# More projection steps between transposes and values in two groups of attention, and the first input tiles loaded among the first weights

## The chip, the cores and the metric

The kernel runs on one core of a Trainium2 chip. The metric is device microseconds of one execution, as the median of several. A profiled execution of the same program gives a trace, with the time and the length of every instruction on each engine. TensorE is written PE (its weight loads PEld), VectorE DVE, ScalarE ACT, GpSimd POOL, and SyncE, which issues most of the transfers here, SP.

## The reference

One layer of a streaming encoder is applied to a prompt of 2048 rows and to a sample of 32 rows that has a cache of 2048 past rows; the model width is 1024. What matters here is its first half:

```
proj = x @ w_in                     # q | k | v | forget logits | B | C | h
logf = log_sigmoid(f_logit + b_f);  c = cumsum(logf)
s = q k^T / 8 + c_q - c_k           # 8 heads of 64, causal
attn = softmax(s) @ v
conv_out = B * dwconv3_causal(C * h)
x = LayerNorm(alpha * x + concat(attn, conv_out) @ w_out)
```

Then follow a gated ConvFFN and a second LayerNorm. Keys, values, log forget values and the states of the convolutions are outputs too. All is fp32.

## The kernel before, in words

**Precision.** A product of fp32 matrices is made of three matmuls: each operand is split into a rounded high half (`hi`, L75 to L82, on ACT, DVE or POOL) and the rest (`lo`, L85, always DVE), and `three` (L87) issues high x high (L89), high x low (L90) and low x high (L91). Tiles are named in pairs: xh and xl (input), wh and wl (weights), ph and pl (probabilities).

**Stages.** The prompt is cut into 4 groups of 512 rows. For each group j, `qkv(j)` (L242) makes keys, queries and values, and `conv(j, half)` (L377) the gated short convolution; `attend(j)` (L528) is the attention of group j's queries over groups 0 to j. `attend_sample`, `cache_gates` and `cache_keys` serve the sample. Then come the output projection with the first norm (`mix`), and the feed-forward. The change touches only the first part, about 0 to 500 us.

**The order by hand.** These functions are Python generators. Each `yield` gives the cost of the stretch just issued, roughly in microseconds of TensorE. `merge` (L1526) drives `together` (L1508): it is given streams with a total each, always resumes the stream with the smallest (cost so far / total), and drops a stream that has ended. So the totals set how fast the streams go against each other: attention in group 0 has the total 24 beside 97 for the projection of group 1, and a yield of 1 in attention lets 97/24 = 4.04 of projection through. What a generator issues between two yields stays together in the program's order; the tile framework may still move an instruction past others where it expects them to wait. Four merges follow each other (L1462 to L1466): group 0's projection alone; attention 0 beside projection 1 and the first cache steps; attention 1 beside projection 2 and the rest of the cache steps; then attentions 2 and 3 with further work.

**A projection step.** `product` (L217) accumulates one 128-column half of a weight piece over the 8 input tiles, and yields 1.3 after every second tile: 6 matmuls of 512 columns. `values` inside `qkv` (L291) yields 1.3 for 12 matmuls of 256 columns. Projection plus `conv(j, 0)` costs 97.1 in all.

**Attention.** For head h and pair 0 or 1 (two blocks of 128 queries each), `scores` (L556) makes score tiles in PSUM, which DVE moves out with the row maximum (L506, L510); `softmax` (L518) takes exp on ACT (L523) and scales on POOL (L525). `values` (L571) then transposes the probabilities on TensorE (`transposed`, L581), splits them (ACT, DVE), and multiplies them by v (L605). The values of a pair come after the scores of the next pair. `nk` is the number of key blocks, 4 j + 2 pair + 2: 2 and 4 in group 0, 6 and 8 in group 1. Up to three sets are transposed ahead (a set is at most four transposes into one PSUM tile), then comes the yield on L593, which the change alters: the merge puts projection there while ACT and DVE make ph and pl. Then each step of values has its own yield (L607).

**The start.** `fetch` (L178) loads, casts and splits the weights in halves of four k tiles. The first half is cut into three transfers (k tile 0, k tile 1, k tiles 2 and 3), in the buffer `wr`. `load_x` (L147) loads the 8 input tiles: for group 0 the first two go into `xr` (2 buffers), the others into the score buffers, which nobody uses yet. All these transfers are issued from SP, one after the other: first the three weight cuts, then the eight tiles, three small constants, then the second half of the weights. TensorE starts with k tile 0.

Of the kernel before, what the change touches and what calls it, by code (L numbers as in the profile page):

```python
# [7 lines left out]
F32 = mybir.dt.float32  # L8
# [9 lines left out]
TS = 32  # L18
# [4 lines left out]
GT = 512  # L23
# [9 lines left out]
def width(j):  # L33
    return GT + TS if j == 0 else GT
# [27 lines left out]
class Kernel:  # L62
# [84 lines left out]
    def load_x(self, j, xp, wide=None):  # L147

        n = width(j)
        self.x = []  # L150
        for k in range(KD):
            if wide and k >= 2:
                if k % 3 == 2:
                    big = wide.tile([128, 2176], F32, tag="p", bufs=5, name="xw")
                r = big[:, n * ((k + 1) % 3):n * ((k + 1) % 3) + n]
            else:
                r = xp.tile([128, GT + TS], F32, tag="xr", bufs=2, name="xr")[:, :n]
            self.dma(r, self.i["xt0"][k] if j == 0 else self.i["xt"][j - 1, k])
            a = xp.tile([128, 640], F32R, tag="xh", bufs=8, name="xh")[:, :n]
            b = xp.tile([128, 640], F32R, tag="xl", bufs=8, name="xl")[:, :n]  # L160
            self.hi(a, r, "act")
            self.lo(b, r, a)
            self.x.append((a, b))
# [14 lines left out]
    def fetch(self, upto):  # L178

        wp = self.wp  # L180
        for s in range(len(self.halves), min(upto, 2 * len(self.order))):
            src, w = self.order[s // 2]
            cuts = [slice(0, 4)] if s else [slice(0, 1), slice(1, 2), slice(2, 4)]
            r = wp.tile([128, 4, 264], F32, tag="wr", bufs=2, name="wr")[:, :, :w]
            a, b = (wp.tile([128, 1152], F32R, tag=t, bufs=3, name=t)[:, :4 * w].rearrange("p (k c) -> p k c", k=4)
                    for t in ("wh", "wl"))
            for c in cuts:
                self.dma(r[:, c], src[:, 4 * (s % 2) + c.start:4 * (s % 2) + c.stop])
                self.hi(a[:, c], r[:, c], "pool" if s else "dve")
                self.lo(b[:, c], r[:, c], a[:, c])  # L190
            self.halves.append([(a[:, k], b[:, k]) for k in range(4)])
# [50 lines left out]
    def qkv(self, j, pools, acc):  # L242
        nc = self.nc
        xp, wp, ev = pools
        n = width(j)
        st = self.stores
        if j == 0:
            self.fetch(1)
        self.load_x(j, xp, None if j else self.at)

# [277 lines left out]
    def attend(self, j, at, mmp, ptp, op):  # L528
# [42 lines left out]
        def values(h, pair, ps, vv):  # L571
            st.flush()
            o = op.tile([128, 256], F32, tag="o", name=f"o{j}o")
            nk = 4 * j + 2 * pair + 2
            def transposed(m):
                last = m == nk // 2 - 1
                pt = ptp.tile([128, GT], F32, tag="pt", name=f"pt{j}t")
                blocks = [(0, 2 * m, 0), (1, 2 * m, 128)]
                blocks += [(1, 2 * m + 1, 256)] if last else [(0, 2 * m + 1, 256), (1, 2 * m + 1, 384)]
                for e, kt, col in blocks:  # L580
                    nc.tensor.transpose(pt[:, col:col + 128], ps[e][:, 128 * kt:128 * kt + 128], self.ident)  # L581
                w = 384 if last else GT
                ph = at.tile([128, GT], F32R, tag="ph", bufs=4, name="ph")
                pl = at.tile([128, GT], F32R, tag="pl", bufs=4, name="pl")
                with self.tc.high_priority(self.HP):
                    self.hi(ph[:, :w], pt[:, :w], "act")
                    self.lo(pl[:, :w], pt[:, :w], ph[:, :w])
                return ph, pl

            nxt = [transposed(0)]  # L590
            for m in range(1, min(3, nk // 2)):
                nxt.append(transposed(m))
            yield 0.43 * len(nxt)  # L593
            for m in range(nk // 2):
                last = m == nk // 2 - 1
                if m + 3 < nk // 2:
                    nxt.append(transposed(m + 3))
                ph, pl = nxt.pop(0)
                order = [(0, ph), (1, ph), (1, pl), (0, pl)]
                for s, (x, pp) in enumerate(order):  # L600
                    kt = 2 * m + x
                    part = last and x == 1
                    oo = o[:, 128:256] if part else o
                    cs = slice(256, 384) if part else slice(256 * x, 256 * x + 256)
                    nc.tensor.matmul(oo, vv[kt // 4][:, kt % 4, :], pp[:, cs],  # L605
                                     start=(m == 0 and s == 0), stop=(last and s == 3))
                yield 0.87 if m + 3 < nk // 2 else 0.43  # L607
            t0 = at.tile([128, 256], F32, tag="ot", bufs=2, name="ot")[:64]
            nc.scalar.copy(t0, o[64:128])
            t1 = at.tile([128, 256], F32, tag="os", bufs=2, name="os")[:64]  # L610
            nc.vector.tensor_tensor(out=t1, in0=o[0:64], in1=t0, op=ALU.add)
            r = slice(64 * (h % 2), 64 * (h % 2) + 64)
            st(self.MX[j][2 * pair:2 * pair + 2, r, h // 2, :].rearrange("t p c -> p t c"),
                     t1.rearrange("p (t c) -> p t c", t=2))
# [813 lines left out]
    def run(self):  # L1428
        tc, nc = self.tc, self.nc
        with ExitStack() as top:  # L1430
# [5 lines left out]
            with ExitStack() as st:  # L1436
                pool = lambda nm, bufs=1, **kw: st.enter_context(tc.tile_pool(name=nm, bufs=bufs, **kw))
                acon = pool("acon")
                self.attention_constants(acon)
                at, ev, xp, wp = pool("at"), pool("ev"), pool("xp"), wpool("wp", bufs=1, side="right")  # L1440
                pools = (xp, wp, ev)
                acon.tile([128, 48], F32, tag="pad", bufs=1, name="pad")
                ev.tile([128, 16], F32, tag="pad", bufs=1, name="pad")
                
                self.at = at
                self.pieces(wp)
                self.stores = Stores(self.dma)
                self.primed = None
                for tag, n in (("p", 5), ("q1", 2), ("k1", 5), ("k2", 5), ("vv", 5), ("ph", 4), ("pl", 4)):
                    at.tile([128, 2176 if tag == "p" else GT], F32, tag=tag, bufs=n, name="at" + tag)  # L1450
                self.q2 = [at.tile([66, GT], F32R, name=f"q2{i}") for i in range(3)]
                for t in self.q2[:2]:
                    nc.gpsimd.memset(t[64:66].bitcast(F32), 1.0)
                mmp = pool("mm", 4, space=PSUM)
                ptp = pool("pt", 3, space=PSUM)
                op = pool("op", 1, space=PSUM)
                acc = lambda: mmp.tile([128, GT], F32, tag="mm", name=f"pm")
                qkv = lambda j: self.qkv(j, pools, acc)
                conv = lambda j, half: self.conv(j, half, pools, acc)
                sample = lambda q: self.attend_sample([q], ev, at, mmp, ptp)  # L1460
                attend = lambda j: self.attend(j, at, mmp, ptp, op)
                merge([(0, [qkv(0), conv(0, 0)])])  # L1462
                merge([(24, [attend(0)]), (97, [qkv(1), conv(1, 0)]), (8, [self.cache_gates(ev, acc), self.cache_keys(ev, (0, 1))])])
                merge([(72, [attend(1)]), (97, [qkv(2), conv(2, 0)]), (12, [self.cache_keys(ev, (2, 3))])])
                merge([(114, [attend(2)]), (150, [qkv(3), together([(44, [sample(0)]), (48, [conv(3, 0)])])])])
                merge([(165, [attend(3)]), (178, [conv(0, 1), together([(44, [sample(1)]), (60, [conv(1, 1), conv(2, 1)])]), conv(3, 1)])])  # L1466
                self.stores.flush()
# [40 lines left out]
def together(streams):  # L1508

    state = [[0.0, total, iter(gens), None] for total, gens in streams]  # L1510
    while state:
        s = min(state, key=lambda s: s[0] / max(s[1], 1))
        try:
            if s[3] is None:
                s[3] = next(s[2])
            cost = next(s[3])
            s[0] += cost
            yield cost
        except StopIteration:
            try:  # L1520
                s[3] = next(s[2])
            except StopIteration:
                state.remove(s)


def merge(streams):  # L1526
    for _ in together(streams):
        pass
# [95 lines left out]
```

## Time and profile before

| | us |
|---|---|
| median of 3 runs | 2678.01 |
| lowest, highest | 2675.28, 2679.25 |
| the profiled execution | 2671.96 |
| its span in the trace | 2670.1 |
| group 0's projection alone (first matmul to the first scores) | 7.7 to 128.4 |
| attention 0 beside projection 1 | 128.4 to about 280 |
| attention 1 beside projection 2 | about 280 to 485 |

The profiled execution is one run of its own; 1.9 us of it lie outside the span. A bracket in a row of the timeline tells how long the engine had been idle before the instruction, and what it waited for. In a row of stretches, the columns are the stretch and its length, the busy time of PE, PEld, DVE, ACT and POOL with the number of instructions, the granted TensorE clock as a share of the full one, the busy share of the DMA engines, and GB/s. Matmuls are pipelined, so the length of one is more than the time from its start to the next one's.

### The profile page before, as it was taken

The numbers are of one execution on the slowest core, as the hardware profiler recorded it, in microseconds if no ns is written. First come the engines' busy times: TensorE is split into PE (matmuls) and PEld (weight loads), VectorE is DVE, ScalarE is ACT, GpSimd is POOL, SyncE is SP. The second block draws the span as 40 slices with busy tenths as digits, with TensorE's granted clock in tenths as the row PEclk, the third lists the DMA queues.
The fourth block names the chain that finished last, engine by engine and source line by source line (L and its number), as shares of the span: only waits on it lengthen the run. The fifth ranks groups of instructions, "written<-read, shape, count | busy, mean of one in ns | idle before, by whom it ended". The sixth has DMA issues, their size and how long they took to land. (4 is left out here: it accounts for less than half of the span.)

```text
span 2670.1 us, 41578 instructions
## 1 busy us (share of the span) xinstructions
PE 2557.1 (96%) x14802; PEld 2213.6 (83%) x14802; DVE 1906.7 (71%) x3610; ACT 1121.1 (42%) x2008; POOL 665.0 (25%) x589
## 2 busy tenths in 40 slices
PE   8999899999999999899999999979899999999998
PEld 8978688788887888688899999956788888888886
DVE  4466666767877777387777777757878877786658
ACT  2142443454544445132444444445544444444442
POOL 2234333232432242100024324343300111111000
PEclk9999899999999999899999999989999999999999
DMA  7777678668647643555534444478764232325765
GB/s 225 199 230 218 200 232 239 192 186 237 196 122 207 184 131 104 164 169 182 198 119 164 154 137 159 155 247 261 244 214 141 103 119 83 111 103 181 246 194 168
DMA packets 350776, 475.09 MB, mean 178 GB/s; under 512 B 42184, under 2 KB 221576, under 8 KB 350568
## 3 DMA queue, kind: packets, MB, share of 16 engines
q1 hardware_dynamic: 348520, 468.64, 56.2%
q10 hardware_dynamic: 2048, 3.80, 0.4%
q8 instruction: 116, 1.90, 0.3%
q14 instruction: 92, 0.75, 0.1%
HBM read 344.22 MB, written 128.11 MB: 177 GB/s over the span
## 5 line engine op out<-in xcount | busy, mean ns | idle before, releaser
L85 DVE TENSOR_TENSOR wp<-wr,wp 128x512 fp32r<-128x512 f32 x550 | 417.9, 781 | 155.8 <-ACT wp L80 151.9
L80 ACT CAST wp<-wr 128x512 fp32r<-128x512 f32 x572 | 339.3, 620 | 266.2 <-PE b L91 179.4
L89 PE MATMUL b<-xt,wp 128*128 128x264 f32 (+1 forms) x1056 | 338.3, 320 | 4.5 <-ACT row L1169 2.4
L90 PE MATMUL b<-xt,wp 128*128 128x264 f32 (+1 forms) x1056 | 337.3, 319 | 0.1
L91 PE MATMUL b<-xt,wp 128*128 128x264 f32 (+1 forms) x1056 | 337.4, 319 | 0.0
L89 PE MATMUL pm<-xh,wh 128*128 128x512 f32 (+1 forms) x800 | 289.5, 363 | 10.4 <-ACT xh L80 8.1
L90 PE MATMUL pm<-xl,wh 128*128 128x512 f32 (+1 forms) x800 | 285.1, 357 | 2.4 <-DVE xl L85 2.3
L91 PE MATMUL pm<-xh,wl 128*128 128x512 f32 (+1 forms) x800 | 284.5, 356 | 1.1 <-DVE wl L85 1.1
L525 POOL TENSOR_SCALAR p<-p,mx 128x128 f32<-128x128 f32 (+15 forms) x128 | 167.8, 1311 | 354.3 <-DVE mx L524 247.6
L89 PE MATMUL b<-xb,wp 128*128 128x264 f32 (+1 forms) x792 | 253.4, 320 | 0.0
L91 PE MATMUL b<-xb,wp 128*128 128x264 f32 (+1 forms) x792 | 253.0, 319 | 0.0
L90 PE MATMUL b<-xb,wp 128*128 128x264 f32 (+1 forms) x792 | 252.8, 319 | 0.0
L90 PE MATMUL b<-wp 128*128 128x512 f32 x616 | 242.7, 394 | 8.8 <-DVE wp L85 8.7
L89 PE MATMUL b<-wp 128*128 128x512 f32 x616 | 240.1, 392 | 4.7 <-ACT wp L80 3.5
L91 PE MATMUL b<-wp 128*128 128x512 f32 x616 | 240.7, 391 | 0.0
L523 ACT ACTIVATE p<-p,mx 128x128 f32<-128x128 f32 (+15 forms) x128 | 154.7, 1209 | 174.7 <-DVE mx L522 173.7
L89 PEld LDWEIGHTS b<-xt,wp 128*128 128x128 f32 x1056 | 198.9, 188 | 19.5 <-ACT row L1169 3.1
L90 PEld LDWEIGHTS b<-xt,wp 128*128 128x128 f32 x1056 | 198.8, 188 | 14.1 <-DVE xt L85 0.4
L91 PEld LDWEIGHTS b<-xt,wp 128*128 128x128 f32 x1056 | 199.0, 188 | 13.7
L1215 POOL TENSOR_TENSOR yx<-row 128x512 f32<-128x512 f32 x22 | 36.5, 1661 | 664.2 <-DVE row L1105 632.5
L89 PEld LDWEIGHTS pm<-xh,wh 128*128 128x128 f32 x800 | 153.5, 192 | 26.8 <-ACT xh L80 8.7
L85 DVE TENSOR_TENSOR wl<-wr,wh 128x1024 fp32r<-128x1024 f32 (+3 forms) x98 | 124.3, 1270 | 69.4 <-POOL wh L78 69.1
(297 smaller groups left out, 5914.3 us busy)
## 6 DMA issues: line engine op xcount, KB each, us to landing
wr<-in_w_mm SPq DMA_DIRECT2D x79, 512.0 KB
wr<-in_w_g SPq DMA_DIRECT2D x44, 512.0 KB
wr<-in_w_val SPq DMA_DIRECT2D x44, 512.0 KB
wr<-tw SPq DMA_DIRECT2D x88, 256.0 KB
k<-ks SPq DMA_DIRECT2D x80, 256.0 KB
vv<-vs SPq DMA_DIRECT2D x80, 256.0 KB
wr<-in_w_down SPq DMA_DIRECT2D x66, 256.0 KB
xr<-in_xt SPq DMA_DIRECT2D x48, 256.0 KB
```

What stands on the lines that cost most here:

```text
L80: nc.scalar.copy(out, in_)
L85: self.nc.vector.tensor_tensor(out=out, in0=in_, in1=hi.bitcast(F32), op=ALU.subtract)
L89: mm(out, sh, mh, start=start, stop=False, **kw)
L90: mm(out, sh, ml, start=False, stop=False, **kw)
L91: mm(out, sl, mh, start=False, stop=stop, **kw)
L523: nc.scalar.activation(p, p, AF.Exp, bias=neg, accum_out=tot)
L525: nc.gpsimd.tensor_scalar(p, p, r, 1.0, op0=ALU.mult, op1=ALU.mult)
L1215: pool = lambda o, x, y, op: nc.gpsimd.tensor_tensor(out=o, in0=x, in1=y, op=op)
```

## The change

Two things are done.

- In the values of attention, the yield between the transposes and the first matmul with v is raised: by 0.87 where nk is 2 and by 0.43 where it is 4 or 6 (first pairs of group 0; second pairs of group 0 and first pairs of group 1). The totals of the two attention streams are raised with it, 24 to 34 and 72 to 79. No instruction is added or removed; the order in which the streams are issued changes.
- The transfers of the first two input tiles are issued among the three cuts of the first weights: cut, tile 0, cut, tile 1, cut. They use the same two `xr` buffers. Their split still comes in `load_x`, which takes the tiles from `self.early`.

```diff
@@ load_x
-            if wide and k >= 2:
+            if wide and k < 2:
+                r = self.early[k]
+            elif wide:
                 if k % 3 == 2:
                     big = wide.tile([128, 2176], F32, tag="p", bufs=5, name="xw")
                 r = big[:, n * ((k + 1) % 3):n * ((k + 1) % 3) + n]
             else:
                 r = xp.tile([128, GT + TS], F32, tag="xr", bufs=2, name="xr")[:, :n]
-            self.dma(r, self.i["xt0"][k] if j == 0 else self.i["xt"][j - 1, k])
+            if not wide or k >= 2:
+                self.dma(r, self.i["xt0"][k] if j == 0 else self.i["xt"][j - 1, k])
@@ fetch
             cuts = [slice(0, 4)] if s else [slice(0, 1), slice(1, 2), slice(2, 4)]
+            firsts = iter(() if s else range(2))
...
             for c in cuts:
                 self.dma(r[:, c], src[:, 4 * (s % 2) + c.start:4 * (s % 2) + c.stop])
+                for k in firsts:
+                    self.raw_x(k)
+                    break
                 self.hi(a[:, c], r[:, c], "pool" if s else "dve")
@@ qkv
         if j == 0:
+            self.early = {}
+
+            def raw_x(k):
+                r = self.early[k] = xp.tile([128, GT + TS], F32, tag="xr", bufs=2, name="xr")[:, :n]
+                self.dma(r, self.i["xt0"][k])
+
+            self.raw_x = raw_x
             self.fetch(1)
@@ attend, values
-            yield 0.43 * len(nxt)
+            yield 0.43 * len(nxt) + (0.87 if nk == 2 else 0.43 if nk <= 6 else 0)
@@ run
-                merge([(24, [attend(0)]), (97, [qkv(1), conv(1, 0)]), (8, [self.cache_gates(ev, acc), self.cache_keys(ev, (0, 1))])])
-                merge([(72, [attend(1)]), (97, [qkv(2), conv(2, 0)]), (12, [self.cache_keys(ev, (2, 3))])])
+                merge([(34, [attend(0)]), (97, [qkv(1), conv(1, 0)]), (8, [self.cache_gates(ev, acc), self.cache_keys(ev, (0, 1))])])
+                merge([(79, [attend(1)]), (97, [qkv(2), conv(2, 0)]), (12, [self.cache_keys(ev, (2, 3))])])
```

## The prediction

> **What bounds the kernel now.** I read the page first: shares of the span.
>
> ```profile
> span 2670.1 us, 41578 instructions
> PE 2557.1 (96%) x14802; PEld 2213.6 (83%) x14802; DVE 1906.7 (71%) x3610; ACT 1121.1 (42%) x2008; POOL 665.0 (25%) x589
> ```
>
> TensorE is the bound. It is idle for 2670.1 - 2557.1 = 113 us, and the change removes no matmul: it can only move idle time and time at a low clock. So the second view is who TensorE waited for:
>
> ```profile
> PE pm L89 <- ACT xh L80: 8.1, 2, 7.7
> PE o0o L605 <- ACT ph L80: 6.5, 4, 3.4
> PE o0o L605 <- DVE pl L85: 2.2, 2, 2.0
> PE s1s L564 <- DVE p L510: 1.9, 1, 1.9
> PE o1o L605 <- DVE pl L85: 0.5, 2, 0.2
> PE o1o L605 <- ACT ph L80: 0.3, 1, 0.3
> ```
>
> The first row is the start (7.7 us until the first matmul). The o0o rows are group 0's values matmuls (L605) waiting for a split half (ph, pl) of the transposed probabilities: 8.7 us. Group 1 (o1o) loses 0.8 us there. Third, the timeline of each place: when the wait ended, and in the bracket how long it was.
>
> ```profile
> 183.39 0.49 PE L581 MATMUL pt0t<-ident,p 128*128 128x128 f32 x3
> 186.21 0.45 PE L605 MATMUL o0o<-ph,vv 128*128 128x256 f32 x2 [0.94 <-ACT ph L80]
> 186.84 0.50 PE L605 MATMUL o0o<-pl,vv 128*128 128x128 f32 x2 [0.17 <-DVE pl L85]
> 222.94 0.49 PE L581 MATMUL pt0t<-ident,p 128*128 128x128 f32 x3
> 226.70 0.45 PE L605 MATMUL o0o<-ph,vv 128*128 128x256 f32 x2 [1.84 <-ACT ph L80]
> 229.18 0.80 PE L605 MATMUL o0o<-pl,vv 128*128 128x128 f32 x2 [2.03 <-DVE pl L85]
> 271.89 0.45 PE L605 MATMUL o0o<-ph,vv 128*128 128x256 f32 x2 [0.35 <-ACT ph L80]
> 279.56 0.80 PE L605 MATMUL o0o<-ph,vv 128*128 128x256 f32 x2 [3.40 <-ACT ph L80]
> 290.19 0.69 PE L581 MATMUL pt0t<-ident,p 128*128 128x128 f32 x2 [2.51 <-POOL p L525]
> ```
>
> Three transposes (x3) are the first pair of a head, where nk is 2. Three of the stalls follow such a set; the 3.40 is a second pair (head 6), and the 2.51 is the last pair. Last, the granted clock by stretch (columns: length, busy time of PE, PEld, DVE, ACT, POOL, then the clock):
>
> ```profile
> 184.00:188.00 4.00, 2.89 (x16) 1.77 (x15) 1.71 (x7) 3.63 (x7) 0.70 (x1) 1.00 0.80 241
> 188.00:192.00 4.00, 4.00 (x25) 3.44 (x23) 2.84 (x10) 0.49 (x2) 0.66 (x1) 1.00 0.87 255
> 230.00:234.00 4.00, 4.00 (x11) 3.17 (x11) 3.14 (x8) 0.86 (x3) 0.89 (x1) 0.50 0.83 240
> 276.20:298.00 21.80, 15.92 (x62) 13.55 (x62) 11.72 (x32) 8.71 (x21) 6.25 (x6) 0.69 0.56 167
> 298.00:485.00 187.00, 176.17 (x1064) 151.90 (x1063) 128.18 (x332) 85.49 (x171) 63.92 (x67) 0.99 0.76 224
> 485.00:500.00 15.00, 12.83 (x50) 9.57 (x48) 10.08 (x29) 4.96 (x8) 3.61 (x3) 0.89 0.63 195
> ```
>
> After the 1.11 us stall near 186 the clock stays at 1.00. After the 1.84 + 2.03 = 3.87 us near 227 it is 0.50: the bill is longer than the wait.
>
> **How the yields become cover.** The merge always steps the stream with the smallest (cost so far / total). So attention's yield of c lets c x 97/24 = 4.04c of projection cost through in group 0 (total 24), 2.85c after (34). A projection step costs 1.3 and is 6 matmuls of 512 columns or 12 of 256. Between transposes and values of a first pair (nk 2): 0.43 x 4.04 = 1.74 before, 1.30 x 2.85 = 3.71 after, so 1.3 steps become 2.9. Second pair (nk 4): 0.86 x 4.04 = 3.48 becomes 1.29 x 2.85 = 3.68, the same. Scores and values, unchanged in cost, get 29% less. Stepping the rule through by its yields, the number of steps at heads 2, 4 and 6, first pair, goes 1, 1, 2 to 2, 3, 3. At head 6, second pair, it goes 0 to 2. Group 0's attention costs 29.24 in all before (8 heads of 1.075 + 0.86 + 1.72) and 39.64 after; when the projection runs out it has done 24/29.24 = 82% and then 34/39.64 = 86%. In group 1, total 72 to 79, first pairs go from 1.29 x 1.35 = 1.74 to 1.72 x 1.23 = 2.11, second pairs down from 1.74 to 1.58; attention's 70.6 (74.04 after) ends at 98% and then 94% of the projection.
>
> **Term 1, stalls under projection: -6.6 us.** A step is 1.4 us of TensorE at full clock:
>
> ```profile
> 180.88 0.40 PE L90 MATMUL pm<-xl,wh 128*128 128x512 f32 x1
> 181.11 0.39 PE L91 MATMUL pm<-xh,wl 128*128 128x512 f32 x1
> 230.20 0.63 PE L90 MATMUL pm<-xl,wh 128*128 128x512 f32 x1
> 230.63 0.63 PE L91 MATMUL pm<-xh,wl 128*128 128x512 f32 x1
> ```
>
> Start to start 0.23 us at clock 1.00 (6 x 0.23 = 1.4) and 0.43 at clock 0.50. Head 2: one more step covers the 1.11, -1.1 (bounds 0 and -1.1). Head 6: -0.35. Head 4: two more steps, 2.8 of the 3.87 us, leave about 1.1. That is as short as the 1.11 us stall, which cost no clock; so the half clock goes too. It lasts for some 12 matmuls (the row of 230 to 234 has 11 in 4 us at 0.50), worth 12 x (0.43 - 0.23) = 2.4 us. Together 5.2. But head 4's cause is not only cover:
>
> ```profile
> 223.55 0.69 DVE L85 TENSOR_TENSOR ckl<-ckf,ckh 128x512 fp32r<-128x512 f32 x1 [4.18 <-DMA kss<-ckl]
> 225.20 0.72 ACT L523 ACTIVATE p<-p,mx 128x512 f32<-128x512 f32 x1 [5.02 <-DVE mx L522]
> ```
>
> VectorE stood 4.18 us before a cache-key split, the score behind it came late, ScalarE's exp (225.20) with it, and ph behind that. By the stepped order this cache step moves from between two scores to behind head 4's transposes, so it no longer precedes that score. Bounds of term 1: 0 (the same block hits another head) and -7.7 (all gone).
>
> The Trainium skill (TensorE: Matmul & The Clock Gate, "HAM oscillation — how this bites in real kernels") puts the limit at TensorE gaps of about 3.4 us; the trace agrees, with half clock after 3.40 and 3.87 and not after 1.11. If the clock were instead lost in proportion to the idle time, 1.1/3.87 of the 2.4 would stay, and term 1 would be -5.9.
>
> **Term 2, the end of group 0: -2.0 us.** From 276.2 to 298 the clock is 0.69 and TensorE idles 5.9 us (21.80 - 15.92). The two steps now behind head 6's second transposes are 2.8 us against its 3.40 us wait: -2.8. But the set of transposes and the scores before it are no longer filler while the next group's x is split: 7 transposes, 1.1 us at most (three in 0.49), I take +0.8. The 2.51 for the last pair stays. Bounds: +3 (the 3.40 comes back at head 7, first pair, without cover) and -11.5 (5.9 idle plus 0.31 x 21.8 = 6.8 of clock, less 1.2 counted twice).
>
> **Term 3, group 1: +0.8 us.** Its second pairs lose a tenth of their cover: I take the o1o rows' 0.8 us once more. Bounds -2 and +3, against 187.00 - 176.17 = 10.8 us idle there.
>
> **Term 4, the end of group 1: +1.4 us.** Attention now ends five steps before the projection instead of one. While group 3's x is split, the last values are missing as filler:
>
> ```profile
> 481.53 0.40 PE L605 MATMUL o1o<-ph,vv 128*128 128x256 f32 x2
> 484.04 0.45 PE L605 MATMUL o1o<-pl,vv 128*128 128x128 f32 x2
> 492.32 0.50 PE L564 MATMUL s2s<-k,q 128*128 128x512 f32 x1 [2.06 <-DVE p L510]
> ```
>
> These are three steps of values, 12 matmuls of 256 columns at half of 0.23, 1.4 us. Bounds 0 and +3.8 (with it the 2.06 us wait becomes 3.5, and a half clock as at 230 adds 2.4).
>
> **Term 5, the start: -1.1 us.** SP issues the two x tiles (each 272 KB) fourth and fifth; after, second and fourth.
>
> ```profile
> 0.79 1.36 SPq L73 DMA_DIRECT2D wr<-in_w_mm  x3
> 2.19 0.94 SPq L73 DMA_DIRECT2D xr<-in_xt  x2
> 6.99 1.33 ACT L80 CAST xh<-xr 128x544 fp32r<-128x544 f32 x2 [4.92 <-DMA xr<-in_xt]
> 7.69 1.05 PE L89 MATMUL pm<-xh,wh 128*128 128x272 f32 x3 [7.69 <-ACT xh L80]
> 9.08 1.13 SPq L73 DMA_DIRECT2D wr<-in_w_mm  x2
> 13.67 1.05 POOL L78 TENSOR_SCALAR wh<-wr 128x1024 fp32r<-128x1024 f32 x1 [7.96 <-DMA wr<-in_w_mm]
> 14.75 1.23 DVE L85 TENSOR_TENSOR wl<-wr,wh 128x1024 fp32r<-128x1024 f32 x1 [1.15 <-POOL wh L78]
> 17.13 0.29 PE L91 MATMUL pm<-xh,wl 128*128 128x272 f32 x1
> ```
>
> Before, the first x lands at 6.97 with 512 KB of weights ahead of it (cuts of 128, 128 and 256 KB; 784 KB in all in 6.2 us from 0.79). After, 128 KB stand ahead of it, 400 KB in all. I estimate 5.4 us, between 4.3 (its share of those bytes in the time) and 6.97. The first matmul would then run near 6.1, 1.6 earlier. What comes next: the second half of the first weights. SP issues it at 9.08, behind all eight x tiles, and the reorder leaves the bytes ahead of it alone; its low half is ready at 14.75 + 1.23 = 15.98. The matmul that needs it ran at 17.13, so at most 1.15 us can be kept: -1.1 (bounds 0 and -1.15). The weight cuts that now land later, behind x, delay nothing unless they come after x itself, whose splits they run beside.
>
> **Sum.** -6.6 - 2.0 + 0.8 + 1.4 - 1.1 = -7.5 us. Against the profiled execution (2671.96 us, span 2670.1) that is 2664.5; this execution was 6.05 below the median 2678.01, so for the median 2670.5. Everything behind 500 us keeps its instructions and only starts earlier.
>
> **Rivals.** *The stalls move.* They are not lack of cover but in-order engines behind late DMAs (the 4.18 us row), and the cache steps, ACT's table loads and the x splits meet other heads. For it: one block made most of term 1. Against it: most first pairs then have three steps, 4.2 us, of cover. Then terms 1 and 2 are about 0 to -1, the rest sums to +1.1: 2677 to 2679, say 2678. Chance 0.28.
>
> *Scores run into VectorE.* With 29% less projection between scores, two score tiles stand back to back more often, and TensorE waits for a score buffer until VectorE has emptied one, as at 492.32 (2.06 us). Place: the eight heads of groups 0 and 1. From 4 such waits (4 x 2.06 = 8.2 us) the gain is gone; eight give 16.5 - 7.5 = +9, 2687; six, +4.9, 2683. For it: VectorE's busy share of 71%. Against it: group 1, whose scores are denser, shows one such wait (the s1s row, 1.9 us). Chance 0.17.
>
> *The yields do nothing,* because the framework orders instructions by modelled times: against it, before's TensorE order has just the stepped one step of projection behind the transposes at heads 2 and 4 (183.39 to the wait's begin at 185.3, and 222.94 to 224.9). It is part of the first rival.
>
> **How the numbers follow.** Forecast 2670.5, chance 0.55. About 0.2%, 5.4 us, is what a measurement of this kernel can tell from no change: faster is below 2672.7, and the forecast is only 2 us past that, so part of its spread falls in "same", as part of the first rival falls in "faster"; these I let cancel. Faster 0.55, same 0.28, slower 0.17. Range: down to 2661 (the good ends of terms 1 and 2, -7.7 and -11.5, with the other three as they are: -18.1, nearly reached), up to 2682 (the first rival whole, the milder third of the second).
>
> **What would show it.** Right: the first matmul near 6.1 us; no o0o wait over 1.5 us before the projection of group 1 ends, and clock 1.00 there; 18 to 36 projection matmuls behind most sets of three transposes. Wrong: o0o or o1o waits of the same total; a first matmul at 6 and L91 of the second half still at 17; new waits of s0s or s1s for VectorE; a half clock near 490 that lasts longer than before.

## The result, and the profile after

The changed kernel takes 2657.28 us in the median of 3 runs (2653.80 to 2661.88), the kernel before 2678.01. The ratio on record is 0.9942 with a 95% interval of 0.9921 to 0.9963: 15.5 us less, between 10 and 21. (The two medians of three runs are 20.7 us apart, at the upper end of that interval; this document counts by the ratio.) The profiled execution took 2657.28 us, with a span of 2655.5. All line numbers of the attention are 14 higher than before (the transposes are L595, the multiplication by v L619).

The page's shares of the span, to set against those quoted in the prediction:

```profile
span 2655.5 us, 41587 instructions
PE 2553.1 (96%) x14802; PEld 2208.5 (83%) x14802; DVE 1908.3 (72%) x3610; ACT 1121.8 (42%) x2008; POOL 665.1 (25%) x589
```

The span is 14.6 us shorter. TensorE's idle time went from 113.0 to 102.4 us, 10.6 less; its busy time fell by 4.0 us with the same 14802 matmuls, so some of them ran faster. The page counts nine instructions more than before, but on none of the five engines listed.

Some of the rows that tell who TensorE waited for (total, times, longest, in us):

```profile
PE pm L89 <- DVE wh L82: 5.6, 1, 5.6
PE o0o L619 <- DVE pl L85: 3.5, 1, 3.5
PE o0o L619 <- ACT ph L80: 2.4, 2, 1.5
PE s1s L578 <- DVE p L524: 0.2, 1, 0.2
PE o1o L619 <- ACT ph L80: 0.3, 1, 0.3
PE o1o L619 <- DVE pl L85: 0.3, 1, 0.3
```

The o0o waits in these rows are 5.9 us instead of 8.7 (one more of 0.34 us stands in the timeline below), the first matmul comes after 5.6 us instead of 7.7. But one wait of 3.5 us is left. The timeline of TensorE shows where it is, with the last waits of group 0 behind it:

```profile
236.12 0.49 PE L595 MATMUL pt0t<-ident,p 128*128 128x128 f32 x3
...
240.31 0.45 PE L619 MATMUL o0o<-ph,vv 128*128 128x256 f32 x2 [0.95 <-ACT ph L80]
244.25 0.80 PE L619 MATMUL o0o<-pl,vv 128*128 128x128 f32 x2 [3.49 <-DVE pl L85]
...
278.05 0.42 PE L619 MATMUL o0o<-ph,vv 128*128 128x256 f32 x2 [1.46 <-ACT ph L80]
279.56 0.80 PE L619 MATMUL o0o<-pl,vv 128*128 128x128 f32 x2 [0.34 <-DVE mx L536]
```

This is head 5, first pair (heads 2, 4 and 6 had the stalls before). Twelve matmuls of projection do stand behind these three transposes, and they were not enough; before, the same set had six behind it and no wait. So too little cover is not the cause here. The timelines of VectorE, GpSimd and ScalarE in the same stretch say why:

```profile
236.18 0.62 POOL L78 TENSOR_SCALAR ckh<-ckf 128x512 fp32r<-128x512 f32 x1 [5.43 <-DMA kss<-ckl]
236.83 1.52 DVE L85 TENSOR_TENSOR ckl<-ckf,ckh 128x512 fp32r<-128x512 f32 x1 [4.47 <-DMA kss<-ckh]
239.05 0.61 ACT L537 ACTIVATE p<-p,mx 128x384 f32<-128x384 f32 x1 [7.14 <-DVE mx L536]
239.78 0.48 ACT L80 CAST ph<-pt0t 128x384 fp32r<-128x384 f32 x1
...
240.47 1.24 DVE L85 TENSOR_TENSOR wl<-wr,wh 128x1024 fp32r<-128x1024 f32 x1
...
242.22 1.51 DVE L85 TENSOR_TENSOR ckl<-ckf,ckh 128x512 fp32r<-128x512 f32 x1 [0.45 <-POOL ckh L78]
243.65 0.54 DVE L85 TENSOR_TENSOR pl<-pt0t,ph 128x384 fp32r<-128x384 f32 x1
```

GpSimd and VectorE stood for 5.43 and 4.47 us at a cache-key split (ckh, ckl) that waited for a store. The score of the next pair, its exp on ScalarE (239.05), and then ph (239.78) came late behind it. pl could have run at 240.3, when ph was there; it ran at 243.65, because a split of the projection's weights (240.47) and a second cache-key split (242.22) stood ahead of it in VectorE's queue. It is the block that the prediction saw at head 4 before, one head further on.

The stretches (length, busy PE, PEld, DVE, ACT, POOL, then granted clock, share of the DMA engines, GB/s), with the half clock that this stall cost in the first row:

```profile
244.20:248.00 3.80, 3.75 (x11) 3.17 (x12) 3.20 (x7) 0.37 (x1) 2.41 (x2) 0.50 0.54 164
274.00:290.00 16.00, 13.12 (x55) 10.23 (x54) 11.92 (x33) 8.20 (x18) 3.78 (x4) 0.79 0.76 234
290.00:472.00 182.00, 174.63 (x1063) 151.89 (x1062) 125.82 (x326) 82.36 (x167) 66.49 (x67) 0.99 0.78 231
472.00:490.00 18.00, 16.85 (x74) 11.58 (x73) 14.94 (x41) 8.91 (x15) 4.09 (x4) 1.00 0.69 202
```

The end of group 0 idles 2.9 us (16.00 - 13.12), where it idled 5.9; group 1 idles 7.4 in 182 us, where it idled 10.8 in 187; behind 472 the clock is 1.00 and the idle 1.15 us, where it was 0.89 and 2.2 us behind 485.

The start, from the timelines of SP, VectorE, TensorE and GpSimd:

```profile
5.28 0.32 DVE L82 CAST wh<-wr 128x256 fp32r<-128x256 f32 x1 [0.59 <-DMA wr<-in_w_mm]
5.62 1.05 PE L89 MATMUL pm<-xh,wh 128*128 128x272 f32 x3 [5.62 <-DVE wh L82]
8.33 0.43 DVE L82 CAST wh<-wr 128x512 fp32r<-128x512 f32 x1 [1.64 <-DMA wr<-in_w_mm]
8.67 0.72 DVE L85 TENSOR_TENSOR xl<-xr,xh 128x544 fp32r<-128x544 f32 x1
9.45 0.59 PE L90 MATMUL pm<-xl,wh 128*128 128x272 f32 x1 [1.42 <-DVE xl L85]
9.79 1.12 SPq L73 DMA_DIRECT2D wr<-in_w_mm  x2
15.11 1.05 POOL L78 TENSOR_SCALAR wh<-wr 128x1024 fp32r<-128x1024 f32 x1 [9.38 <-DMA wr<-in_w_mm]
19.05 0.39 ACT L276 COPY kf<-pm 128x272 f32<-128x272 f32 x1 [5.77 <-PE pm L91]
```

The first matmul is 2.07 us earlier. Then 1.42 us go to a wait: the third weight cut landed late, its cast held VectorE until 8.3, and the low half of the second input tile stood behind it. The second half of the first weights was issued at 9.79 (before 9.08) and cast at 15.11 (before 13.67). In both traces SP's first eight issues wait for nothing, and each of the 9th to the 15th waits for the landing of the transfer eight places before it. The second half is the 15th and waits for the 7th, an input tile that landed at 9.77 (before 9.06). The first keys leave PSUM at 19.05; before, at 18.59.

Milestones of the two profiled executions, each the first matmul of its kind, set the stages against the terms:

| stretch | before | after | difference | predicted |
|---|---|---|---|---|
| start to first scores of group 0 | 128.4 | 128.5 | +0.1 | -1.1 (term 5) |
| to first values of group 1 | 176.5 | 166.9 | -9.6 | -8.6 (terms 1, 2) |
| to first scores of group 2 | 180.8 | 177.4 | -3.4 | +0.8 (term 3) |
| to first values of group 2 | 20.3 | 18.4 | -1.9 | +1.4 (term 4) |
| to the end of the span | 2164.1 | 2164.3 | +0.2 | 0 |

In the second stretch, where most of the gain lies, TensorE idles 10.3 us instead of 14.1 and runs at half clock for 13.7 us instead of 20.5. The idle time gives 3.8 of the 9.6 us; the 6.8 us less of half clock are worth up to 3.4, an estimate that takes a matmul as twice as long there (0.43 beside 0.23 us from start to start).

Such differences of two single executions are rough. The second stretch, with its order of group 0 unchanged, took 176.5, 173.1 and 172.1 us in three profiles of different kernels; the third, with group 1's order unchanged, 178.3 to 185.4 in six. Only the timed experiments decide what each part is worth.

### The profile page after: what moved, and what is told of

Its sections match the earlier page's. It is cut to its first block, busy times and chain, and to the rows that moved or that the text cites. A ratio compares the mean times of both kernels' runs of the same rounds, so it can differ in the third digit from the quotient of the medians.

```text
span 2655.5 us, 41587 instructions
## 1 busy us (share of the span) xinstructions
PE 2553.1 (96%) x14802; PEld 2208.5 (83%) x14802; DVE 1908.3 (72%) x3610; ACT 1121.8 (42%) x2008; POOL 665.1 (25%) x589
## 5 line engine op out<-in xcount | busy, mean ns | idle before, releaser
L91 PE MATMUL b<-xt,wp 128*128 128x264 f32 (+1 forms) x1056 | 337.7, 320 | 0.0
L91 PE MATMUL pm<-xh,wl 128*128 128x512 f32 (+1 forms) x800 | 282.9, 355 | 1.5 <-DVE wl L85 1.5
L91 PE MATMUL b<-xb,wp 128*128 128x264 f32 (+1 forms) x792 | 252.7, 319 | 0.0
L91 PE MATMUL b<-wp 128*128 128x512 f32 x616 | 240.8, 391 | 0.0
L91 PEld LDWEIGHTS b<-xt,wp 128*128 128x128 f32 x1056 | 199.3, 189 | 13.8
```

The source lines that it names most:

```text
L91: mm(out, sl, mh, start=False, stop=stop, **kw)
```

## The experiments

The theory after the result: the early tiles bring nothing; the new order brings all; part of it is more projection under the splits, part is group 0's attention lasting longer, so that less of it is left without projection. The rival: the stalls only move, and what was gained is a matter of which heads they meet.

**One part alone.** Four kernels, each before with one part of the change.

```diff
 e1_tiles_only: the diff of load_x, fetch and qkv; yields and totals as before
 e2_yields_only: yield and both totals of the change; no early tiles
 e3_group0_only:
-            yield 0.43 * len(nxt)
+            yield 0.43 * len(nxt) + (0.87 if nk == 2 else 0.43 if nk <= 4 else 0)
-                merge([(24, [attend(0)]), ...
+                merge([(34, [attend(0)]), ...
 e4_group1_only:
-            yield 0.43 * len(nxt)
+            yield 0.43 * len(nxt) + (0.43 if nk == 6 else 0)
-                merge([(72, [attend(1)]), ...
+                merge([(79, [attend(1)]), ...
```

> Only the early loading of the two input tiles; yields and totals as before. The changed kernel's trace has its first matmul 2.1 us earlier, but its first scores at 128.5 us where the kernel before had them at 128.4. Theory (the second half of the first weights, issued behind all input tiles, sets the pace from about 15 us on): first matmul near 5.6 us, first scores within 0.3 us of 128.4, time within 2 us of the kernel before. Rival (the start does gain and something between 20 and 128 us happened to give it back): first scores 1 to 2 us early here, or the time 2 to 4 us lower.

> Only the yields and the totals (34, 79) of both groups; loading as before. If the tiles bring nothing: the same ratio as the whole change, 0.994, some 12 to 20 us below the kernel before, with the first scores of group 2 about 13 us earlier than before. If the tiles are a part of the gain: 1 to 4 us worse than the whole change.

> Yields and total of group 0's attention alone (0.87 and 0.43, total 34); group 1 as before, tiles as before. Read from the traces of the kernels before and after, group 0 with its end gives 9.5 us. Theory (cover and a shorter end in group 0 do most of it): 8 to 11 us below before. Rival (both groups need each other, or it is luck of where the cache steps fall): under 5 us.

> Yield of group 1's first pairs (0.43) and total 79 alone; group 0 and tiles as before. The prediction had a loss here (+0.8 +1.4 = +2.2 us); the traces of before and after show 5.3 us gained from the first values of group 1 to those of group 2 (3.4 up to the first scores of group 2, 1.9 behind). If that gain is the edit's own: 3 to 6 us below before. If it came from how group 0 hands over: within 2 us of before or slower.

The column of us is the ratio's, on the median of the kernel before in the same session (2673.29 us here, 2674.27 in the next table).

| kernel | ratio to before | 95% interval | us |
|---|---|---|---|
| the early tiles alone | 1.0009 | 0.9993 to 1.0025 | +2.4 |
| yields and totals alone | 0.9948 | 0.9930 to 0.9966 | -13.9 |
| of these, group 0's alone | 0.9964 | 0.9949 to 0.9978 | -9.6 |
| of these, group 1's alone | 0.9998 | 0.9983 to 1.0014 | -0.5 |

The tiles are worth nothing and the order is worth the whole. (With the tiles alone the first scores ran at 129.9 us, not within 0.3 of 128.4 as expected; nothing was gained by them.) Group 0's share, -9.6, is the larger one. Group 1's edit alone does nothing that can be measured. With group 0's it adds 4.3 us (13.9 - 9.6), but the two intervals overlap, so that this addition is likely and not proven. One execution can't settle it either: group 1's stretch took 177.3 us with both edits and 181.2 with group 0's alone, but 186.6 with group 1's edit alone, where nothing came of it.

**Cover or pace.** Group 0's edit does two things: the yield puts more projection behind the transposes (cover), the total slows attention against the projection (pace). Three kernels, before with these lines:

```diff
 e5_total34_no_yield:   merge([(34, [attend(0)]), ...   yields as before
 e6_yield_total24:      merge([(24, [attend(0)]), ...   yields of e3
 e7_yield_total40:      merge([(40, [attend(0)]), ...   yields of e3
```

> Group 0 only: total 34 instead of 24, the yields left as before; tiles and group 1 as before. By the merge rule nearly every set of transposes then has 1 or 2 steps of projection behind it (as before or one less), but attention ends 11 steps ahead of the projection, so no transposes or values stand without projection (before, the last 3 sets do). Theory (cover behind the transposes makes the gain): the waits of o0o stay at 5 us or more and the time is within 3 us of the kernel before, or slower. Rival (most of group 0's gain is its end, where attention ran alone while the next input tiles were split): 5 to 9 us below before.

> Group 0 only: yields raised (0.87, 0.43), total left at 24. By the merge rule every set up to head 4 has 4 steps of projection behind it, and the projection runs out there: five and a half of 16 pairs then run with no projection. Cover theory for the first part: no o0o wait over 1 us up to head 4. What the end without projection costs: with the end of the kernel before (three pairs alone, about 11 us lost) as the measure, twice as many pairs should lose some 20 us, and the time is 5 to 12 us above before; if the end costs nothing of its own, the time is below before.

> Group 0 only: yields raised, total 40, so that attention (39.6) and projection end together: 2 or 3 steps behind every set, none without projection. If both cover and the end count, this is at least as good as total 34 with the same yields (ratio 0.9964): 9 to 15 us below before. If the gain of total 34 came from the third step of cover, it is smaller: 3 to 7 us below.

| kernel | ratio to before | 95% interval | us |
|---|---|---|---|
| pace alone (total 34) | 0.9976 | 0.9966 to 0.9987 | -6.4 |
| cover alone (total 24) | 0.9964 | 0.9953 to 0.9976 | -9.6 |
| cover, total 40 | 0.9979 | 0.9968 to 0.9991 | -5.6 |
| cover, total 34 (above) | 0.9964 | 0.9949 to 0.9978 | -9.6 |

Each alone gives most of the gain, and both together no more than the cover alone. So they do not add. The total of 40 gives less, but its interval overlaps that of 34. Two expectations missed: the cover theory had the pace alone within 3 us of the kernel before, and the theory that cover and end both count had the total of 40 at least as good as 34. Had an end of attention without projection a cost of its own, the cover with the old total should have been slower by it than the same with 34; it was not, and that part of the theory falls. The waits of the cover alone, from TensorE's timeline, show that the stalls have changed their places:

```profile
223.70 0.50 PE L89 MATMUL pm<-xh,wh 128*128 128x512 f32 x1 [2.45 <-POOL wh L78]
226.17 0.80 PE L91 MATMUL pm<-xh,wl 128*128 128x512 f32 x1 [1.74 <-DVE wl L85]
...
272.86 0.77 PE L564 MATMUL s0s<-k,q 128*128 128x128 f32 x2 [5.04 <-DMA q<-qh]
```

The o0o waits are 0.5 us in all, but the projection waits for its own weights' split at 223.70 and 226.17, and at 272.86 scores stand 5.04 us for the load of a query. The first two have the cause seen above: on GpSimd and VectorE the weights' split stands behind a cache-key split (222.02 and 222.67), before which they had been idle for 4.67 and 4.80 us. In the pace alone, the waits of group 0 by their causes:

```profile
PE pt0t L581 <- POOL p L525: 4.9, 3, 2.2
PE o0o L605 <- ACT ph L80: 4.4, 3, 2.5
PE o0o L605 <- DVE pl L85: 0.9, 4, 0.3
```

With mostly one or two steps of cover there are still 10.2 us of waits, where before had 8.7 of o0o and 2.5 for the last pair; but the longest is 2.54 us, and the mean clock from the first scores to the first values of group 1 is 0.99, where it was 0.94: waits spread out cost less clock, though not none (four stretches of this kernel stand in the last section). With the total 40, a longer wait is back, at head 7:

```profile
272.94 0.58 PE L605 MATMUL o0o<-pl,vv 128*128 128x128 f32 x2 [2.62 <-DVE pl L85]
```

**The cause of the long stall.** The stall is no accident of one execution: the five profiles with the change's order in group 0 all have it at head 5, with 3.49 or 3.50 us before pl, and the three with the order of before have it at head 4, with 2.03 us. If the block at heads 4 and 5 is the cache-key step, taking that step out of group 0's merge must remove it, with the change otherwise whole.

```diff
 e8_cache_keys_later (to the changed kernel):
-  merge([(34, [attend(0)]), ..., (8, [self.cache_gates(ev, acc), self.cache_keys(ev, (0, 1))])])
-  merge([(79, [attend(1)]), ..., (12, [self.cache_keys(ev, (2, 3))])])
+  merge([(34, [attend(0)]), ..., (8, [self.cache_gates(ev, acc)])])
+  merge([(79, [attend(1)]), ..., (24, [self.cache_keys(ev, (0, 1, 2, 3))])])
 e9_cache_keys_one_merge_on (to the changed kernel):
+  merge([(34, [attend(0)]), ..., (8, [self.cache_gates(ev, acc)])])
+  merge([(79, [attend(1)]), ..., (12, [self.cache_keys(ev, (0, 1))])])
+  merge([(114, [attend(2)]), ..., (12, [self.cache_keys(ev, (2, 3))])])
```

> The whole change, and the first eight cache-key steps moved out of group 0's merge into group 1's (16 steps there, total 24). In the changed kernel one stall is left in group 0: 4.4 us idle at head 5's values, and half clock after it, with VectorE standing 4.5 us before a cache-key split. Theory (an in-order VectorE behind a cache step makes the long stall, not too little projection): no o0o wait over 2 us and clock 1.00 from 150 to 270 us, the last values of group 0 some 6 us earlier than in the changed kernel; what it costs in group 1 is open, 0 to 6 us. Rival (two steps of cover are too few for any first pair): a stall of 2 us or more stays at a first pair with two steps.

> The whole change, and each batch of eight cache-key steps one merge later: heads 0 to 3 from group 0's merge into group 1's (total 12, as that merge had before), heads 4 to 7 from group 1's into group 2's (total 12). Moving all of the first batch on top of the second gave group 0 back about 11 us up to the first values of group 1 (156 us from the first scores instead of 167) and lost 24 us in group 1 (202 us to the first scores of group 2 instead of 177). Theory (a cache step blocks VectorE and GpSimd in order, and eight of them per group are bearable, sixteen not): group 0 stays at 156 +- 3 us, group 1 returns to 177 +- 5 us, group 2 pays 0 to 6 us; time 5 to 11 us below the whole change, ratio 0.990 to 0.992. Rival (group 1's loss came from how group 0 ends, not from the number of steps): group 1 stays above 190 us and the time is no better than the whole change.

All four steps in group 1's merge: ratio 1.0004 (0.9991 to 1.0016), the whole gain is gone. One merge on each: 0.9978 (0.9963 to 0.9993), 5.9 us less than before, where the change has 15.5 less. What the step costs where it goes was underrated both times: 0 to 6 us had been expected in group 1, and a time below that of the change for the second. In the stretches of the first, group 0 and then group 1:

```profile
128.40:267.80 139.40, 136.06 (x815) 116.74 (x813) 94.22 (x251) 56.45 (x136) 50.60 (x60) 1.00 0.73 219
267.80:486.10 218.30, 196.09 (x1119) 166.96 (x1117) 143.37 (x362) 90.30 (x182) 74.34 (x76) 0.95 0.75 221
```

Group 0 idles 3.3 us at a clock of 1.00. In the changed kernel it is 145.5 us with 6.9 idle:

```profile
128.50:274.00 145.50, 138.56 (x812) 118.24 (x811) 98.08 (x254) 55.26 (x133) 54.02 (x65) 0.98 0.77 226
```

So the cache-key step is the cause of the long stall: with it gone, and the same number of projection matmuls behind each set of transposes up to head 6, group 0 has no o0o wait over 0.52 us. Up to the first values of group 1 that gives 10.9 us (156.0 instead of 166.9), 4.9 of them idle time, and none of the 13.7 us of half clock is left. But group 1 idles 22.2 us, and from its first values to the first scores of group 2 it takes 201.8 us instead of 177.4, 24 more. With each step one merge on, group 0, 1 and 2:

```profile
128.70:267.20 138.50, 136.16 (x816) 116.89 (x814) 94.11 (x251) 56.52 (x136) 50.45 (x60) 1.00 0.73 221
267.20:466.60 199.40, 185.16 (x1118) 160.66 (x1116) 133.51 (x355) 89.86 (x182) 70.20 (x69) 0.98 0.73 215
466.60:711.20 244.60, 232.20 (x1400) 197.78 (x1398) 175.66 (x441) 115.76 (x199) 81.13 (x82) 0.99 0.77 220
```

Group 0 is as good as in the first, and group 1 near its time in the change (182.7 us from first values to the first scores of group 2, beside 177.4). Now group 2 pays: 244.6 us, where the change has this row:

```profile
472.80:707.40 234.60, 228.72 (x1400) 196.65 (x1398) 170.94 (x434) 115.48 (x199) 75.95 (x75) 1.00 0.71 206
```

Group 2 idles 12.4 us instead of 5.9, and behind it another 9 us go (1957.1 to the end of the span, beside 1948.1); of these only a part can be the edit's, since with nothing changed there the other profiles have 1948.0 to 1955.2. Among group 2's waits, the sample's scores now stand for the keys of the cache, a row that the change does not have in this stretch:

```profile
PE ss L676 <- DMA k1s<-kss: 4.4, 3, 2.8
PE s2s L578 <- DVE p L524: 3.8, 7, 1.2
```

The rival, that the stalls move, is right about this block: taken out of group 0, where it cost 11 us, it costs 10 to 24 us where it goes. It is wrong about the edit as a whole: the five timed kernels that have group 0's yield, its total or both, and leave the cache steps in their merges, are all faster than before, by 5.6 to 13.9 us, though the stalls stand at different places in them.

**The start.** Two kernels for term 5, each run once: the changed kernel with the third cut cast on GpSimd, and with that, the second half of the first weights issued ahead of tile 4.

```diff
 e10_third_cut_on_gpsimd (to the changed kernel):
-                self.hi(a[:, c], r[:, c], "pool" if s else "dve")
+                self.hi(a[:, c], r[:, c], "pool" if s or c.start == 2 else "dve")
 e11_second_half_before_tile4 (to e10), in load_x's loop over k:
+            if wide and k == 4:
+                self.fetch(2)
```

> The whole change, and the third cut of the first weights cast on GpSimd instead of VectorE. In the changed kernel TensorE starts at 5.6 us but idles 1.4 us until 9.45 for the low half of tile 1: VectorE stands before the cast of the third cut, which lands at 8.3, while tile 1 has been there since 6.9. Theory: that idle time goes (low half of tile 1 by 7.7 us), and yet the first keys leave no earlier than 18 us (17.8 to 19.1 in seven runs without the early tiles, 18.3 to 19.5 in three with them), because the second half of the first weights still lands near 14.5 to 15. Rival (this idle time is what ate the early start): first keys out near 17.0 us.

> As the run with the third cut on GpSimd, and besides the second half of the first weights is issued before input tiles 4 to 7 instead of behind all eight. Theory (the landing of that half sets when the first keys leave): it lands near 10 us instead of 14 to 15, and the first keys leave between 14.5 and 17 us. Rival (the low clock of the first 5 to 7 us, or the last input tiles, which now land near 15 us, set it): first keys still at 18 us or later.

They took 2661.64 and 2663.68 us in one execution each, beside 2673.12 of the kernel before on that chip, in the median of 12; neither is told apart from the change by that. The profile is what counts here. With the third cut on GpSimd, from the timelines of TensorE, GpSimd and ScalarE:

```profile
7.73 0.59 PE L90 MATMUL pm<-xl,wh 128*128 128x272 f32 x1 [0.17 <-DVE xl L85]
15.03 1.05 POOL L78 TENSOR_SCALAR wh<-wr 128x1024 fp32r<-128x1024 f32 x1 [5.02 <-DMA wr<-in_w_mm]
18.94 0.39 ACT L276 COPY kf<-pm 128x272 f32<-128x272 f32 x1 [5.68 <-PE pm L91]
```

The 1.42 us wait is 0.17, and the first keys come at 18.94 all the same, because the second half of the weights is cast at 15.03 as before. With that half issued earlier:

```profile
11.10 1.04 POOL L78 TENSOR_SCALAR wh<-wr 128x1024 fp32r<-128x1024 f32 x1 [2.12 <-DMA wr<-in_w_mm]
13.06 0.68 DVE L85 TENSOR_TENSOR wl<-wr,wh 128x512 fp32r<-128x512 f32 x1
13.79 0.39 PE L91 MATMUL pm<-xh,wl 128*128 128x272 f32 x1 [1.43 <-DVE wl L85]
17.39 0.39 ACT L278 COPY kf<-pm 128x272 f32<-128x272 f32 x1 [2.89 <-PE pm L91]
```

The cast comes 3.9 us earlier and the first keys only 1.55: now the low half of the third cut (13.06) stands behind input tiles in VectorE's queue, and a new wait of 1.43 us comes of it. (17.39 is also a little outside the 14.5 to 17 expected.) And the 1.55 us do not last: the first scores of group 0 run at 133.8 us here, at 132.1 in the kernel before this one, and at 128.5 in the change. So the second half of the weights does set when the first keys leave. Whether the start sets the end of the stage these two single profiles can't tell: the first scores come between 127.3 and 133.8 us in all thirteen, and both kernels lose a stretch of half clock on the way (at 81.5 and at 37.6 us) that the change does not have.

## Why the prediction was right or wrong

**Bound, and where the gain lies: right.** TensorE's work is the same, idle time and clock moved. The change is faster, as the likeliest case had it; but by 15.5 us (10 to 21) and not 7.5, so the sum is about 8 us short. 2678.01 less 15.5 is 2662.5, just inside the range, whose lower end is 2661; the measured median itself, 2657.28, lies below it.

**Steps of the merge: right.** Behind the first sets of three transposes stand 16, 24, 12, 18, 36, 12 and 18 projection matmuls in heads 0 to 6, where 16, 18, 6, 12, 12, 6 and 12 stood before. The predicted 18 to 36 holds for four of seven; at head 7 only one matmul stands there. Behind head 6's second set there are 12, the predicted two steps, where there were none.

**Term 1 (-6.6), wrong in its content.** Heads 2, 4 and 6 lost their stalls as said. The step that failed is the one that let head 4's stall and its half clock go for good: it gave head 4 two more steps of cover and moved the cache-key split out of its way, and went on as if the block were gone. It met head 5, with 0.95 + 3.49 = 4.44 us and a half clock of the same length. "No o0o wait over 1.5 us, clock 1.00" was wrong. The bound 0 had named exactly this ("the same block hits another head"), and I had put the value near the other end. The step to "the half clock goes too", from a rest of 1.1 us, was not put to the test, since the rest was 4.44.

**Term 2 (-2.0), too small.** The end of group 0 idles 2.9 us instead of 5.9, at 0.79 in place of 0.69. The 3.40 us wait of head 6 went, as said. Two steps failed. "The 2.51 for the last pair stays": it is gone, and new waits came at head 7 (1.08, 1.46 and 0.34 us). And the value held no clock at all, only the bound did: by the two rows, 21.80 us at 0.69 and 16.00 us at 0.79, the time at half clock fell from 13.5 to 6.7 us (the traces' clock records know full and half clock alone). Cut at the last projection matmul of group 1 (273.95 and 272.06 us), the two profiles give -2.0 for what stands before it, most of term 1, and -7.6 behind it up to the first values of group 1, and their sum is -9.6 beside -8.6. The timed kernel with group 0's edit alone also gives -9.6 (-6 to -14). A right sum of two wrong halves.

**Terms 3 and 4 (+0.8, +1.4), wrong in sign.** I took the longer attention as a loss of cover for second pairs and of filler at the end. In the profile, o1o waits went from 0.8 to 0.6 us, s1s waits from 1.9 to 0.2, and the clock behind group 1 rose to 1.00. Alone the edit costs nothing (-0.5, between -4.5 and +3.7), so +2.2 is not excluded for it alone; behind group 0's edit it comes with a gain of some 4 to 6 us (13.9 or 15.5, less 9.6), which the intervals allow to be as little as nothing. From its first scores to those of group 2, group 1 idles 10.3 us instead of 13.3 in the two profiles, and TensorE is busy 188.3 instead of 191.8. What makes that gain stays open: a better handover from group 0, or chance in where stalls fall. The early half clock that I feared near 490 did not come.

**Term 5 (-1.1), wrong.** The first matmul came at 5.62, better than the 6.1 predicted. The step that failed is the conclusion from "the reorder leaves the bytes ahead of it alone": the bytes are the same, but SP's issue waits for the landing of the fourth input tile, and that came at 9.77 instead of 9.06. So the second half of the weights was issued 0.7 us and cast 1.4 us later. Why the same bytes took longer to land was not found. (The lower bound for the first tile, 4.3, does not follow from the figures given: 400/784 of 6.2 us behind 0.79 is 3.9; nothing else hangs on it.) In the seven profiles without the early tiles that cast starts at 13.7 to 14.5 us (mean 14.0) and the first keys come out at 18.3 in the mean, in the five with them at 14.4 to 15.1 (mean 14.9) and 19.0. Besides, I had overlooked that VectorE takes the third cut's cast ahead of the second tile's low half. Measured, the part is worth +2.4 us (-1.9 to +6.7): nothing. The sign that would show it wrong, L91 of the second half still at 17, is what came: 17.47.

**The rivals.** *The stalls move*: true of the cache-key block, in three kernels, and not of the whole. *Scores run into VectorE*: no. The s1s waits for a score buffer fell from 1.9 to 0.2 us, and s0s has one of 0.3.

## What to carry to other kernels

Where a stall has a cause that can be named, ask first where that cause goes, and only then whether the cover suffices: here a step that makes a queue wait for a transfer stood in front of something in each of the orders tried, and a price of 10 to 24 us went with it from stage to stage. Judge a reordering by timed kernels with one part each: the stalls of a stage reshuffle with every edit, single profiles of one order differ by 4 to 7 us, and two edits that give 6.4 and 9.6 us alone gave 9.6 together. And two input tiles brought forward paid nothing here, since the transfer that is next in the chain was pushed back.

## What the hardware showed

The half clock comes after shorter stalls than I had thought, and not after each. It followed 1.84 + 2.03 us before and 0.95 + 3.49 us in the change, both broken by two matmuls, and 2.45 + 1.74 us in the cover alone; but also the single 2.62 us of the total 40 (projection matmuls then start 0.43 us apart for 2.6 us). In the pace alone, a wait of 2.15 us for transposes that ended at 212.1 cost the clock, and one of 2.54 us for ph that ended at 261.4 did not, as these stretches of it show, each 3.41 us long:

```profile
208.90:212.31 3.41, 1.25 (x8) 0.83 (x7) 1.48 (x7) 1.29 (x6) 2.57 (x4) 1.00 0.74 199
212.31:215.72 3.41, 3.41 (x12) 2.83 (x11) 1.32 (x3) 1.03 (x3) 0.55 (x2) 0.50 0.65 201
256.68:260.09 3.41, 2.18 (x11) 1.44 (x10) 3.41 (x10) 0.00 (x0) 1.30 (x1) 1.00 0.71 147
260.09:263.50 3.41, 1.94 (x9) 1.42 (x10) 3.25 (x7) 2.10 (x6) 2.41 (x2) 1.00 0.79 260
```

So the length of the gap alone does not decide. The clock records of the traces tell what does. Up to 500 us the thirteen traces hold 46 half clocks, each 3.41 or 6.83 us long, and in each trace all of them begin on one grid of 3.41 us. Of the stretches of this grid at full clock, every one in which TensorE was busy for less than 0.47 of the time was followed by half clock, none in which it was busy for more than 0.65, and between the two it went either way. The 2.15 us lie in one such stretch and leave it 1.25 us of work (0.37). The 2.54 us, from 258.87 to 261.41, are cut in two by the grid and leave 0.64 and 0.57. So the same wait can cost nothing, or 3.41 us and more at half clock, by where it falls on the grid. The 3.4 us that the prediction took from the Trainium skill (TensorE: Matmul & The Clock Gate, "HAM oscillation — how this bites in real kernels") is no bound for a single gap in these runs: 2.15 us was enough once.

At the start, matmuls of 272 columns run 0.226 us apart and later 0.125, while the granted clock's column shows 1.00: the trace has no clock record there, and the column takes that as full clock. The first record, of full clock, comes where the slow period ends: at 12.7 us before and at 13.2 in the change, where TensorE had begun 2.1 us sooner; at 11.7 with the yields alone and at 14.2 with the tiles alone, at 13.2 with the third cut on GpSimd and at 10.3 with the second half ahead of tile 4, these two with the first matmul at 4.95 and 4.97. Over the thirteen profiles it lasted from 3.1 us (10.9 - 7.8, the cover alone) to 8.6 us (14.25 - 5.69, the tiles alone), and an earlier first matmul did not buy an earlier full pace. The Trainium skill (TensorE: Matmul & The Clock Gate, "Part 1: The HAM clock gate") speaks of a window that runs freely of the kernel, so that the end varies; these runs agree. It gives about 3.4 us of sustained work for the slow part; here it was 3.1 to 8.6 us from the first matmul, waits included.
